# Rounding residues of queries and keys: VectorE for both heads in a hybrid decoder step

## The chip, the cores and the metric

The kernel runs on one core of one Trainium2 chip. The metric is device time in microseconds of one execution of the whole program, from the first instruction to the last; lower is better.

## What is computed

One inference step of a two-layer decoder trunk on 1024 prompt positions and 8 sample positions (1032 columns in all), width 1024, in float32. The first layer mixes tokens with dilated sliding-window attention in three groups of 16 heads, the second with causal pooling; each is followed by a gated MLP with a short convolution. The change lies in the attention of the prompt, which the reference computes per group so:

```python
s = jnp.einsum("nbqhd,nbkhd->nbhqk", qb, kb).astype(jnp.float32) * SCALE
s = s + bias[:, np.clip(rel, 0, SPAN)]
s = jnp.where(valid[None, :, None], s, NEG_INF)
m = jnp.max(s, axis=-1)
p = jnp.exp(s - m[..., None])
l = jnp.sum(p, axis=-1)
o = jnp.einsum("nbhqk,nbkhd->nbqhd", p.astype(v.dtype), vb).astype(jnp.float32)
```

The three groups' outputs are then merged per head, weighted by their softmax denominators, projected and added to the input.

## The kernel before

Activations lie with channels on partitions and positions along the free dimension. Every large product is made of three matmuls in a rounded format (`F32R`): a value is split into a rounded part (hi, a cast) and what the rounding left (lo, a subtraction), and hi x hi, hi x lo and lo x hi are accumulated. Weights are split by `w_split` (L104 cast on ScalarE, L109 subtraction, in the attention stage on GpSimd, in two pieces of 512 columns).

The attention stage runs over 24 units: 8 head pairs, and for each the groups 2, 1, 0. While unit n's queries, keys and values are projected (three weights times three chunks of columns, `accumulate`, L129), unit n-1's attention is woven between the matmuls. A plan of (due time, step) pairs sets the order; its clock is moved by `between()`, once after every three matmuls. Scores (`scores`) are due every 6 ticks from 1, transposes of the exponentials (`probs_t`) from 15, the value product (`pv`) from 24. Each engine works its own queue in order, so the place in the plan is the place in the queue.

What `probs_t` makes is called phl: TensorE transposes the exponentials into the one PSUM bank `pt` (L484, L486), ScalarE casts them (L488), VectorE subtracts (L489). The next transposes need the bank empty, and `pv` (L498, writes `o`) needs phl.

`pack_q` and `pack_k` split a unit's queries and keys for the next unit's scores. A head pair shares 128 partitions, A (the first head, h = 0) the lower 64, B (h = 1) the upper 64. Each works in halves of 512 columns and per head, so each is four steps: `pack_q` is due at 29 and 32 (first half) and at 44.5 and 46.5, `pack_k` at 50, 53, 56 and 59 of the unit's 72 ticks. A step of `pack_q` casts (L407 on ScalarE for the first head, L406 on VectorE for the second) and subtracts (L408); one of `pack_k` casts on VectorE (L417), copies the cast for the other half of the partitions on ScalarE (L418) and subtracts (L419). In the traces the queries are named `x` (the program's own rows `x0`, `x1` are used for them), `x_595` for the first head and `x_596` for the second, the keys `k`.

Other work shares these queues. In the units of an odd head pair (counted from 0) the cached keys of the sample positions are multiplied on GpSimd (L655, `kc`) and summed on VectorE (L644, `sc`); in those of the following even pair the cached values are split (L795 on ScalarE, L796 on GpSimd) and multiplied (L778, `spv`, gathered in `so`, L805). When a head pair's last group is done, `Merge` computes the groups' weights on VectorE (L578 to L586, `me`), TensorE transposes them (L591, `mt`), and GpSimd scales and adds the groups' outputs (L612, L614), in the units of groups 2 and 1 of the next pair. `finish_o` (L534) adds the value products into the output on VectorE. L380 copies the sample columns out of a projection's bank.

Of the kernel before, what the change touches and what calls it, by code (L numbers as in the profile page):

```python
# [11 lines left out]
F32 = mybir.dt.float32  # L12
# [35 lines left out]
def trunk(ctx: ExitStack, tc: tile.TileContext, a, out):  # L48
    nc = tc.nc
# [102 lines left out]
    def x_row(k, dtype=F32):  # L152
        return persist.tile([128, NT], dtype, name=f"x{k}", tag=f"x{k}")
# [137 lines left out]
    with ExitStack() as ph:  # L291
# [9 lines left out]
        keys = [qp.tile([128, 2, T], F32R, name=f"k{h}") for h in range(2)]  # L301
# [95 lines left out]
        queries = []  # L397

        def pack_q(u):

            raw = u.raw[0]
            if not queries:
                queries.extend(x_row(h, F32R)[:, :T] for h in range(2))

            def part(h, own, other, t):
                (nc.vector.tensor_copy(queries[h][own, t], raw[own, t]) if h else  # L406
                 nc.scalar.activation(queries[h][own, t], raw[own, t], AF.Copy))  # L407
                (nc.vector if h else nc.gpsimd).tensor_sub(queries[h][other, t], raw[own, t],  # L408
                                                           queries[h][own, t].bitcast(F32))

            return parts(part, (0, T // 2))

        def pack_k(u):
            raw = u.raw[1]

            def part(h, own, other, t):
                nc.vector.tensor_copy(keys[h][own, 0, t], raw[own, t])  # L417
                nc.scalar.activation(keys[h][other, 0, t], raw[own, t], AF.Copy)  # L418
                (nc.vector if h else nc.gpsimd).tensor_sub(keys[h][own, 1, t], raw[own, t],  # L419
                                                           keys[h][own, 0, t].bitcast(F32))  # L420


            return parts(part, (T // 2, 0))

        def parts(f, starts):
            return [partial(f, h, own, other, slice(t, t + T // 2)) for t in starts
                    for h, (own, other) in enumerate(((A, B), (B, A)))]
# [994 lines left out]
```

## Time and profile before

| what | value |
|---|---|
| median of 3 runs | 2860.18 us (2855.91 to 2860.97) |
| profiled execution | 2860.84 us, span 2859.0 us |
| TensorE (PE) matmul busy | 2778.1 us, 97% of the span |
| VectorE (DVE) busy | 1606.4 us, 56% |
| ScalarE (ACT) busy | 1362.1 us, 48% |
| GpSimd (POOL) busy | 1102.1 us, 39% |
| mean granted TensorE clock | 0.991 |

The shares are means over stages: the attention stage is about the first 1160 us, the rest is projection, pooling and the MLPs. A busy time counts the whole length of an instruction, including time in which it stands still for something that another engine holds. Idle time before an instruction is shown in brackets with what ended it.

### The profile page before, as it was taken

The page shows a single profiled execution, that of the slowest core. Times are in us where ns is not written, and L with a number is a line of the kernel's source. Part 1 is how long each engine was busy: PE and PEld are TensorE (multiplying, and loading weights), DVE is VectorE, ACT ScalarE, POOL GpSimd, SP SyncE. Part 2 cuts the span into 40 slices and gives each one's busy share as a digit, 9 for nine tenths or more (in the row PEclk, how much of TensorE's full clock was granted, in tenths as well). Part 3 has the DMA queues.
Part 4 walks back from the last instruction along what each step waited for, and adds up shares of the span by engine and source line. Part 5 has one row for each costly group of instructions (what it writes and reads, how often), then busy time and mean ns, then how long its engine had stood idle before and what let it go on. Part 6 is the DMA issues. An engine that isn't in the chain of part 4 may idle for free. (4 is left out here: it accounts for less than half of the span.)

```text
span 2859.0 us, 46821 instructions
## 1 busy us (share of the span) xinstructions
PE 2778.1 (97%) x18109; PEld 2741.0 (96%) x18109; DVE 1606.4 (56%) x3335; ACT 1362.1 (48%) x2748; POOL 1102.1 (39%) x982
## 2 busy tenths in 40 slices
PE   7999999999999999999999999999999999999998
PEld 6999999999999999889999999999999999999998
DVE  6566766676666666765333234787755334346655
ACT  5565665566656665634223323445542233334443
POOL 4335453545354535545444443011143443431110
PEclk9999999999999999999999999999999999999999
DMA  3234332433343324437222222333422226223542
GB/s 116 62 83 127 89 98 74 137 88 97 76 136 86 98 74 147 150 93 107 74 67 74 67 68 80 111 118 118 135 87 67 70 73 78 67 75 116 170 144 91
DMA packets 203950, 277.80 MB, mean 97 GB/s; under 512 B 70272, under 2 KB 154096, under 8 KB 203728
## 3 DMA queue, kind: packets, MB, share of 16 engines
q1 hardware_dynamic: 203680, 274.80, 34.3%
q8 instruction: 142, 2.33, 0.3%
q14 instruction: 80, 0.66, 0.1%
q10 hardware_dynamic: 48, 0.02, 0.0%
HBM read 251.89 MB, written 23.34 MB: 96 GB/s over the span
## 5 line engine op out<-in xcount | busy, mean ns | idle before, releaser
L129 PE MATMUL mm<-hh,w_hi 128*128 128x352 f32 (+2 forms) x4064 | 1342.7, 330 | 11.8 <-DVE x L1010 3.8
L129 PE MATMUL mm<-hl,w_hi 128*128 128x352 f32 (+2 forms) x4064 | 1306.4, 321 | 3.9 <-DVE hl L264 2.8
L129 PE MATMUL mm<-hh,w_lo 128*128 128x352 f32 (+2 forms) x4064 | 1306.9, 322 | 2.4 <-DVE w_lo L109 2.4
L129 PEld LDWEIGHTS mm<-hh,w_hi 128*128 128x128 f32 x4064 | 771.2, 190 | 18.4 <-ACT hh L260 4.3
L129 PEld LDWEIGHTS mm<-hl,w_hi 128*128 128x128 f32 x4064 | 772.2, 190 | 5.7 <-DVE hl L264 4.0
L129 PEld LDWEIGHTS mm<-hh,w_lo 128*128 128x128 f32 x4064 | 770.1, 189 | 3.3 <-DVE w_lo L109 3.3
L109 POOL TENSOR_TENSOR w_lo<-w_raw,w_hi 128x512 fp32r<-128x512 f32 (+1 forms) x294 | 532.8, 1824 | 565.5 <-ACT w_hi L104 564.1
L104 ACT ACTIVATE w_hi<-w_raw 128x1024 fp32r<-128x1024 f32 x348 | 364.7, 1050 | 292.1 <-PE mm L129 266.2
L1124 DVE SCALAR_TENSOR_TENSOR conv<-gate,convp,conv 128x336 f32<-128x336 f32 (+1 forms) x176 | 220.4, 1252 | 385.0 <-ACT conv L1122 375.9
L129 PE MATMUL mm<-gh,w_hi 128*128 128x352 f32 (+2 forms) x1056 | 340.6, 322 | 4.0 <-ACT gh L1115 2.1
L129 PE MATMUL mm<-gh,w_lo 128*128 128x352 f32 (+2 forms) x1056 | 339.9, 322 | 2.0 <-DVE w_lo L109 2.0
L129 PE MATMUL mm<-gl,w_hi 128*128 128x352 f32 (+2 forms) x1056 | 340.0, 322 | 0.3 <-POOL gl L1116 0.3
L1062 DVE TENSOR_TENSOR x<-x,mm 128x352 f32<-128x352 f32 (+2 forms) x312 | 157.0, 509 | 226.6 <-PE mm L129 225.9
L476 ACT ACTIVATE p<-p,st 128x128 f32<-128x128 f32 (+1 forms) x384 | 170.0, 443 | 195.9 <-DVE st L473 195.2
L1116 POOL TENSOR_TENSOR gl<-conv,gh 128x352 fp32r<-128x352 f32 (+2 forms) x132 | 123.4, 937 | 339.4 <-ACT gh L1115 336.5
L109 DVE TENSOR_TENSOR w_lo<-w_raw,w_hi 128x1024 fp32r<-128x1024 f32 x136 | 166.5, 1225 | 87.8 <-ACT w_hi L104 87.8
L129 PEld LDWEIGHTS mm<-gh,w_hi 128*128 128x128 f32 x1056 | 199.8, 189 | 4.6 <-ACT gh L1115 2.4
L129 PEld LDWEIGHTS mm<-gh,w_lo 128*128 128x128 f32 x1056 | 200.3, 190 | 2.2 <-DVE w_lo L109 2.2
L129 PEld LDWEIGHTS mm<-gl,w_hi 128*128 128x128 f32 x1056 | 199.9, 189 | 0.7 <-POOL gl L1116 0.7
L489 DVE TENSOR_TENSOR phl<-pt,phl 128x512 fp32r<-128x512 f32 (+1 forms) x192 | 104.6, 545 | 165.8 <-ACT phl L488 164.7
L377 ACT ACTIVATE raw<-mm 128x336 f32<-128x336 f32 (+1 forms) x216 | 145.0, 671 | 102.6 <-PE mm L129 97.5
L1107 ACT ACTIVATE gate<-mm 128x352 f32<-128x352 f32 (+2 forms) x132 | 60.2, 457 | 261.8 <-PE mm L129 261.8
(190 smaller groups left out, 3104.6 us busy)
## 6 DMA issues: line engine op xcount, KB each, us to landing
w_raw<-in_w_in SPq DMA_DIRECT2D x176, 512.0 KB
w_raw<-in_w_out SPq DMA_DIRECT2D x88, 512.0 KB
w_raw<-in_w_qkv SPq DMA_DIRECT2D x72, 512.0 KB
x<-qd SPq DMA_DIRECT2D x48, 256.0 KB
kc<-in_cache_k SPq DMA_DIRECT2D x48, 256.0 KB
vc<-in_cache_v SPq DMA_DIRECT2D x48, 256.0 KB
x<-c_d SPq DMA_DIRECT2D x42, 256.0 KB
out_new_k<-raw SPq DMA_DIRECT2D x8, 516.0 KB
```

The costliest lines, as they stand in the source:

```text
L104: nc.scalar.activation(hi, raw, AF.Copy)
L109: eng.tensor_sub(lo[:, s:s + step], raw[:, s:s + step], hi[:, s:s + step].bitcast(F32))
L129: nc.tensor.matmul(ps, l, r, start=first and i == 0, stop=last and i == n - 1)
L377: nc.scalar.activation(stream(raw[:, :T], u.g, c0, t1, which > 0), ps[:, :w].rearrange("p (s r) -> p s r", r=DILS[u.g]), AF.Copy, scale=si ...
L476: nc.scalar.activation(p[:, h, :w], p[:, h, :w], AF.Exp, bias=u.st[:, i, h, 0:1], scale=-1.0, accum_out=u.st[:, i, h, 1:2])
L489: nc.vector.tensor_sub(phl[:, :, 1, :w], ps[:, :, :w], phl[:, :, 0, :w].bitcast(F32))
L1062: nc.vector.tensor_add(xT[ct][:, c0:c1], xT[ct][:, c0:c1], ps)
L1107: nc.scalar.activation(gate[:, 2 + s:2 + e], group(tiles8(w, c), c), AF.Copy)
L1116: nc.gpsimd.tensor_sub(self.gl[f][:, s:e], conv[:, s:e], self.gh[f][:, s:e].bitcast(F32))
L1124: nc.vector.scalar_tensor_tensor(conv[:, :n], gate[:, j:j + n], cw[j], conv[:, :n], op0=ALU.mult, op1=ALU.add)
```

## The change

The subtractions of the first head in `pack_q` and `pack_k`, 48 and 48 of them, are issued on VectorE instead of GpSimd. The casts stay where they were.

```diff
             def part(h, own, other, t):
                 (nc.vector.tensor_copy(queries[h][own, t], raw[own, t]) if h else
                  nc.scalar.activation(queries[h][own, t], raw[own, t], AF.Copy))
-                (nc.vector if h else nc.gpsimd).tensor_sub(queries[h][other, t], raw[own, t],
-                                                           queries[h][own, t].bitcast(F32))
+                nc.vector.tensor_sub(queries[h][other, t], raw[own, t], queries[h][own, t].bitcast(F32))
...
                 nc.vector.tensor_copy(keys[h][own, 0, t], raw[own, t])
                 nc.scalar.activation(keys[h][other, 0, t], raw[own, t], AF.Copy)
-                (nc.vector if h else nc.gpsimd).tensor_sub(keys[h][own, 1, t], raw[own, t],
-                                                           keys[h][own, 0, t].bitcast(F32))
+                nc.vector.tensor_sub(keys[h][own, 1, t], raw[own, t], keys[h][own, 0, t].bitcast(F32))
```

The order on TensorE, ScalarE and the DMA queue is the same in both; line numbers past L408 are one or two lower in the changed kernel. VectorE's queue, while the queries' second half and the keys of the last head pair's group 1 are packed (the stretch from 1101 us), before (`sc` is the sums of the sample's scores, `k_100` the first head's keys, `k_101` the second's):

```order
L534 TENSOR_TENSOR x_12532<-o,part 64x4x64 x2
L489 TENSOR_TENSOR phl<-pt,phl 128x2x128
L380 TENSOR_SCALAR ks<-mm 128x8
L406 CAST x_596<-raw 64x512
L408 TENSOR_TENSOR x_596<-raw,x_596 64x512
L644 TENSOR_REDUCE sc<-kc 128x2x2 x2
L417 CAST k_100<-raw 64x512
L489 TENSOR_TENSOR phl<-pt,phl 128x2x128
L417 CAST k_101<-raw 64x512
```

and now:

```order
L532 TENSOR_TENSOR x_12532<-o,part 64x4x64 x2
L408 TENSOR_TENSOR x_595<-raw,x_595 64x512
L487 TENSOR_TENSOR phl<-pt,phl 128x2x128
L380 TENSOR_SCALAR ks<-mm 128x8
L406 CAST x_596<-raw 64x512
L408 TENSOR_TENSOR x_596<-raw,x_596 64x512
L642 TENSOR_REDUCE sc<-kc 128x2x2 x2
L416 CAST k_100<-raw 64x512
L418 TENSOR_TENSOR k_100<-raw,k_100 64x512
L487 TENSOR_TENSOR phl<-pt,phl 128x2x128
L416 CAST k_101<-raw 64x512
```

A subtraction of the first head now stands ahead of each phl subtraction.

GpSimd's queue in the same stretch, before:

```order
L614 TENSOR_TENSOR x_10954<-x_10954,x_11970 128x512
L655 TENSOR_TENSOR kc<-kc,x_12437 128x512
L408 TENSOR_TENSOR x_595<-raw,x_595 64x512
L109 TENSOR_TENSOR w_lo<-w_raw,w_hi 128x512 x2
L655 TENSOR_TENSOR kc<-kc,x_12437 128x512
L419 TENSOR_TENSOR k_100<-raw,k_100 64x512
L655 TENSOR_TENSOR kc<-kc,x_12437 128x512
L419 TENSOR_TENSOR k_100<-raw,k_100 64x512
```

and now:

```order
L612 TENSOR_TENSOR x_10954<-x_10954,x_11970 128x512
L653 TENSOR_TENSOR kc<-kc,x_12437 128x512
L109 TENSOR_TENSOR w_lo<-w_raw,w_hi 128x512 x2
L653 TENSOR_TENSOR kc<-kc,x_12437 128x512 x2
L109 TENSOR_TENSOR w_lo<-w_raw,w_hi 128x512 x4
```

The weight split and the cache products close up behind one another; the second weight split, which waits for ScalarE, follows.

## Rows read from the trace of the kernel before

**Rows 1.** TensorE's waits, 85 to 1160 us: waiter, waited for; total us, times, longest.

```profile
PE mt L591 <- DVE me L586: 8.4, 4, 2.1
PE spv L778 <- DVE so L805: 5.9, 6, 1.4
PE o L498 <- DVE phl L489: 5.1, 5, 2.0
PE pt L484 <- DVE phl L489: 1.9, 5, 0.5
```

**Rows 2.** The two changed lines: engine, count; ns min/median/max; first and last start; form.

```profile
L408 POOL TENSOR_TENSOR x<-raw,x x48: 1275/1288/1717, 64.0 to 1145.6; 64x512 fp32r<-64x512 f32 x48
L408 DVE TENSOR_TENSOR x<-raw,x x48: 686/687/1673, 65.6 to 1147.3; 64x512 fp32r<-64x512 f32 x48
...
L419 POOL TENSOR_TENSOR k<-raw,k x48: 1266/1450/1752, 72.0 to 1157.6; 64x512 fp32r<-64x512 f32 x48
L419 DVE TENSOR_TENSOR k<-raw,k x48: 687/1652/1679, 72.4 to 1160.1; 64x512 fp32r<-64x512 f32 x48
```

**Rows 3.** Timeline from 1101 us, VectorE, GpSimd, TensorE: start, length, operation [idle before].

```profile
1101.38 0.42 DVE L489 TENSOR_TENSOR phl<-pt,phl 128x256 fp32r<-128x256 f32 x1 [0.38 <-ACT phl L488]
...
1102.25 0.47 DVE L406 CAST x<-raw 64x512 fp32r<-64x512 f32 x1
1102.76 1.66 DVE L408 TENSOR_TENSOR x<-raw,x 64x512 fp32r<-64x512 f32 x1
...
1105.09 0.76 DVE L417 CAST k<-raw 64x512 fp32r<-64x512 f32 x1
1105.77 0.41 DVE L489 TENSOR_TENSOR phl<-pt,phl 128x256 fp32r<-128x256 f32 x1
...
1111.71 0.42 DVE L489 TENSOR_TENSOR phl<-pt,phl 128x256 fp32r<-128x256 f32 x1
...
1101.15 1.28 POOL L612 TENSOR_TENSOR x<-x,x 128x512 f32<-128x512 f32 x1
1102.51 1.35 POOL L614 TENSOR_TENSOR x<-x,x 128x512 f32<-128x512 f32 x1
1103.83 1.74 POOL L655 TENSOR_TENSOR kc<-kc,x 128x512 f32<-128x512 f32 x1
...
1107.08 3.07 POOL L109 TENSOR_TENSOR w_lo<-w_raw,w_hi 128x512 fp32r<-128x512 f32 x2
...
1106.68 0.38 PE L484 MATMUL pt<-consts,p 128*128 128x128 f32 x2
...
1112.19 0.55 PE L498 MATMUL o<-phl,vhl 128*128 128x128 f32 x3 [0.41 <-DVE phl L489]
```

**Rows 4.** Timeline from 395 us, VectorE, GpSimd, TensorE, columns as above.

```profile
396.21 1.40 DVE L417 CAST k<-raw 64x512 fp32r<-64x512 f32 x1
397.54 0.41 DVE L489 TENSOR_TENSOR phl<-pt,phl 128x256 fp32r<-128x256 f32 x1
...
395.71 3.05 POOL L109 TENSOR_TENSOR w_lo<-w_raw,w_hi 128x512 fp32r<-128x512 f32 x2
...
398.01 0.44 PE L484 MATMUL pt<-consts,p 128*128 128x128 f32 x2 [0.20 <-DVE phl L489]
```

**Rows 5.** Busy us by stretch: PE, PEld, DVE, ACT, POOL, granted clock; one wait.

```profile
197.00:211.00 14.00, 11.93 (x81) 11.64 (x80) 13.22 (x29) 7.39 (x14) 8.30 (x6) 0.99 0.37 110
289.00:305.00 16.00, 16.00 (x110) 15.96 (x109) 15.18 (x27) 8.68 (x20) 11.28 (x10) 1.00 0.32 93
439.00:451.00 12.00, 12.00 (x83) 11.99 (x82) 9.34 (x13) 5.99 (x14) 4.82 (x4) 1.00 0.26 68
...
210.60:214.00 3.40, 3.40 (x14) 3.40 (x14) 1.57 (x8) 2.47 (x7) 1.50 (x2) 0.50 0.43 163
...
209.49 0.29 PE L591 MATMUL mt<-consts,me 128*48 128x128 f32 x1 [2.07 <-DVE me L586]
```

**Rows 6.** The first unit's keys, timeline of VectorE and TensorE.

```profile
72.43 1.63 DVE L419 TENSOR_TENSOR k<-raw,k 64x512 fp32r<-64x512 f32 x1
...
74.21 0.55 PE L464 MATMUL s<-k,x 128*128 128x256 f32 x1 [0.26 <-DVE k L419]
```

## The prediction

> **What bounds the kernel now.** I read first the busy time by stretch, then what TensorE waits for, then the instructions around those waits. Between 439 and 451 us TensorE is busy for all of 12.00 us [rows 5]: in the attention stage, from 85 to 1160 us, where the changed lines run, it is the bound, so a delay elsewhere costs time only when TensorE reaches a matmul whose operand isn't ready. The list of TensorE's waits in that stage is short: 8.4 us in four waits for the merge weights, 5.9 us for the sample sums, 5.1 and 1.9 us for the rounded probabilities (phl), all made by VectorE [rows 1]. None is for GpSimd's subtractions. So taking those off GpSimd opens nothing on TensorE's path in this stage; what counts is whether VectorE, which already ends every wait, gets later.
>
> It has little room. In a unit of an odd head pair it is busy 13.22 of 14 us, or 15.18 of 16, while keys are packed; in a unit of an even pair without sample or merge work 9.34 of 12 [rows 5].
>
> **Price of one subtraction.** The four rows of the two lines say it [rows 2]: on GpSimd 1.28 us at best, 1.29 and 1.45 in the median; on VectorE 0.69 at best, but up to 1.68, and the key line's median is 1.65. The long ones are those that start while a GpSimd operation runs: the two engines take turns. In the unit at 394 us the cast at 396.21 takes 1.40 us behind the first piece of GpSimd's weight split (two pieces from 395.71 in 3.05 us), where a cast alone takes 0.47 [rows 3, 4]. The order is by turns too: when VectorE finishes one such instruction and GpSimd has one waiting, GpSimd goes next (the cast of 1102.25 ends at 1102.72, GpSimd's operation of 1102.51 then runs to 1103.86, and the subtraction behind the cast, from 1102.76, takes 1.66 us [rows 3]). So the 96 moved subtractions cost VectorE between 0.69 and 0.69 + 1.28 us each, and what they give back is the wait that GpSimd's own subtraction used to cause, up to 1.68 - 0.69 = 0.99 us each. One at a time that is anything from -0.3 to +2.0 us; the place decides, by what VectorE has next in its queue and what GpSimd has ready.
>
> The Trainium skill, "SBUF — State Buffer", section "Who interferes with whom", says that a VectorE instruction with two inputs in SBUF and a GpSimd instruction that reads SBUF share a port, which the one that comes first holds for its whole length while the other blocks. The rows at 396.21 agree. The page alone would also speak for this change: 0.69 us of holding replaces 1.28; that result is the second rival below.
>
> **The change, place by place.** Each of the 24 units (a head pair and a group) has four subtractions of the first head: two query halves and two key halves. The first query half comes some 10 us before the rest; the other three fall into the crowded stretch. The program's order on TensorE, ScalarE and the DMA queue stays; on VectorE each first-head subtraction is put directly behind its cast, ahead of the phl subtraction that TensorE waits for.
>
> *Odd pairs, group 1 (four units).* I walk the one at 1101 us [rows 3]. Now: phl done at 1101.80; second query cast done 1102.72; its subtraction 1104.42; first key cast 1105.85; phl 1106.18, half a microsecond ahead of the transposes at 1106.68, which need that PSUM bank empty. Then: the new query subtraction takes its turn before GpSimd's operation of 1101.15, ends at 1101.9, phl at 1102.35. GpSimd's operation slides to 1103.2, the cast behind it ends at 1103.6 (0.9 late); GpSimd's next takes until 1104.9, the second head's subtraction ends at 1105.6 (1.2 late); the cache product of 1103.83 now runs to 1106.9, the key cast ends at 1107.3 (1.5 late). The weight split is next and takes its first piece, to 1108.6; only then the new key subtraction, to 1109.3, and phl, to 1109.7: 3.5 us late, 3.0 more than TensorE's slack. At the next phl (now done at 1112.13, with a wait of 0.41) the second new key subtraction and one more GpSimd turn make VectorE 4.3 us late in all. The walk gives +4.3; I take 3.5, since it has every GpSimd operation ready the moment the removed ones leave its queue, and some need a transfer. 4 x 3.5 = 14.0 us.
>
> *Even pairs after the first, group 1 (three units).* Now: cast until 397.61, phl until 397.95, transposes at 398.01 already wait 0.20 [rows 4]. Then: behind the cast the second weight piece goes first (1.28), to 398.9; the new subtraction ends at 399.6, phl at 400.0. 2.0 us late, nothing in between: 3 x 2.0 = 6.0 us.
>
> *Odd pairs, group 2 (four units).* The merge weights stand on VectorE right behind the key packing, and TensorE already waits 2.07 us for them at 209.49 [rows 5]. Two new key subtractions come ahead of them; I let the waits saved and the waits added cancel: 2 x 0.69 = 1.4, four times: 5.6 us.
>
> *Odd pairs, group 0 (four units).* No wait now, at 15.18 of 16 us busy [rows 5]. The same two subtractions find no room: 4 x 1.4 = 5.6 us.
>
> *The rest.* In units like that at 439 us three subtractions, 2.1 us, fit into 12 - 9.34 = 2.7 us of idle time: nothing. The units with sample products I put at nothing too; they have idle time at the places where the new ones stand.
>
> *The first unit.* Here TensorE does wait for the packing: its second score matmul starts at 74.21, when VectorE's 1.63 us subtraction of 72.43 is done [rows 6]. With GpSimd out of the way both heads' take 2 x 0.69 = 1.4: -0.3 us.
>
> A new wait comes with the move: VectorE, in order, now waits for ScalarE's cast of the first head's queries before it subtracts, and phl, the second head's cast and the score reductions queue behind it. That cast stands ahead of the one that phl itself waits for on ScalarE, so I price it at nothing; if it came last, it would add to the group 1 units.
>
> Sum: 14.0 + 6.0 + 5.6 + 5.6 - 0.3 = 30.9 us. The profiled execution took 2860.84 us (span 2859.0), 0.7 above the median of 2860.18: about 2891 us by the median, 1.1% slower.
>
> **Rivals.** *Worse than that.* The walk's full 4.3 in group 1 of the odd pairs, and in all seven group 1 units the first query half makes one more turn, 1.0 us: 4 x (4.3 + 1.0) + 3 x (2.0 + 1.0) = 30.2 in place of 20.0. On top, TensorE's clock: after the 2.07 us wait at 209.49 the granted clock in 210.6 to 214.0 is 0.50, the level of 1.2 GHz [rows 5], so 1.7 us of its work is lost; seven new waits of some 2 us would add 12. Together 2860 + 31 + 10 + 12 = 2913 us. For it: the turns are in the rows. Against it: not every wait of 2 us need bring the clock down, and a slow TensorE gives VectorE time. Chance 0.15.
>
> *Faster.* One mechanism: in the crowded stretches the shared turns, not VectorE's own work, set when VectorE is done, and a removed GpSimd subtraction gives back 0.97 us (1.66 against 0.69 in the second head's query subtraction at 1102.76 [rows 3]) for 0.69 spent. Then three per unit gain 0.84 us in the 15 units above: -12.6, well within TensorE's waits of 21.3 us [rows 1], so 2847 us. It decides from the point where a removed subtraction saves VectorE more than 0.69 us on average. Against it: GpSimd has other work ready in its place (from 1101.15 on its operations follow with hardly a gap), so the turn isn't given back but taken by the next operation. The port rule of the page named above would put the gain higher, since it compares 1.28 with 0.69; the rows speak for the turn being used by others. Chance 0.10.
>
> *No difference.* Given back and spent cancel within 0.2% (5.7 us, about what a measurement of this kernel can tell from no change): if only the even pairs' group 1 units lose, 2860 + 6 - 0.3 = 2866, or less. It needs VectorE's lateness to be made good before TensorE asks; the half microsecond of slack at 1106.18 speaks against it. Chance 0.12.
>
> **How the numbers follow.** Forecast 2891 us, chance 0.63, with its own range from 2867 (0.2% above, where each unit loses what its slack lets through) to 2905. Range: 2861 leaves out the faster case and a little of the second; 2914 takes in the worse case's sum. Faster by over 0.2%: 0.10; within: 0.12; slower: 0.63 + 0.15 = 0.78.
>
> **What would show it.** In the changed kernel's trace: VectorE's subtractions of both lines, 96 each, GpSimd's gone; TensorE's waits for phl, now 7.0 us in ten, over 20 us, with waits of 2 to 4 us at the transposes of group 1 units; the four waits for merge weights near 3.5 us each, in one piece or shared with a wait for phl just ahead; no new wait in even pairs' group 0. If TensorE's waits for phl stay near 7 us while VectorE's busy time in the crowded stretches doesn't grow, the turns were given back and the forecast is wrong. If VectorE waits for ScalarE's query cast for more than a few microseconds in all, I priced that at nothing wrongly.

## The result, and the profile after

The changed kernel takes 2876.09 us in the median of four runs (2874.05 to 2881.04), against 2859.18 us for four runs of the kernel before beside it: a ratio of 1.006, 95% interval 1.0044 to 1.0076. It is slower by 0.6%, 17 us; the forecast was 31 us. The profiled execution took 2874.05 us with a span of 2872.2 us, 13.2 more than the span of before; where the other 4 us of the medians' distance lie no trace shows.

TensorE's waits in the attention stage, 85 to 1175 us of the changed kernel (waiter, what it waited for; total us, times, longest), against [rows 1]:

```profile
PE pt L482 <- DVE phl L487: 19.5, 19, 2.4
PE spv L776 <- DVE so L803: 7.1, 6, 1.8
PE o L496 <- DVE phl L487: 4.8, 5, 1.9
PE mt L589 <- DVE me L584: 3.1, 4, 0.8
```

(Line numbers after the change are one or two lower than before.) The waits for phl at the transposes have gone from 1.9 us to 19.5; the four for the merge weights have fallen from 8.4 us to 3.1. The two changed lines, now VectorE's alone (count; ns min/median/max), and what VectorE waited for ahead of the first, against [rows 2]:

```profile
L408 DVE TENSOR_TENSOR x<-raw,x x96: 684/687/1797, 64.1 to 1160.9; 64x512 fp32r<-64x512 f32 x96
its engine sat idle before it (us, times) until:
  ACT x L407: 5.2, 15
...
L418 DVE TENSOR_TENSOR k<-raw,k x96: 682/690/1675, 71.6 to 1173.2; 64x512 fp32r<-64x512 f32 x96
```

The key subtraction's median was 1652 ns before and is 690 now. The engines' busy time (page of the changed kernel):

```profile
PE 2779.5 (97%) x18109; PEld 2738.2 (95%) x18109; DVE 1645.1 (57%) x3431; ACT 1363.3 (47%) x2748; POOL 980.8 (34%) x886
```

VectorE has 96 instructions more and is busy 38.7 us longer (1606.4 before), 0.40 us for each new one, less than the 0.69 us that one takes alone. So part of the new work was paid by waits that VectorE no longer has. A unit with merge weights shows it instruction by instruction. First the kernel before, from 196.9 us (start, length, operation): the four key casts of VectorE with their subtractions, then GpSimd.

```profile
197.49 1.01 DVE L417 CAST k<-raw 64x512 fp32r<-64x512 f32 x1
199.13 0.81 DVE L417 CAST k<-raw 64x512 fp32r<-64x512 f32 x1
199.97 1.67 DVE L419 TENSOR_TENSOR k<-raw,k 64x512 fp32r<-64x512 f32 x1
203.18 1.13 DVE L417 CAST k<-raw 64x512 fp32r<-64x512 f32 x1
204.80 1.15 DVE L417 CAST k<-raw 64x512 fp32r<-64x512 f32 x1
205.99 0.69 DVE L419 TENSOR_TENSOR k<-raw,k 64x512 fp32r<-64x512 f32 x1
...
201.06 1.74 POOL L419 TENSOR_TENSOR k<-raw,k 64x512 fp32r<-64x512 f32 x1
204.39 1.27 POOL L419 TENSOR_TENSOR k<-raw,k 64x512 fp32r<-64x512 f32 x1 [0.36 <-DVE k L417]
```

Then the same unit of the changed kernel, VectorE, GpSimd and TensorE:

```profile
196.99 0.96 DVE L416 CAST k<-raw 64x512 fp32r<-64x512 f32 x1
197.99 1.68 DVE L418 TENSOR_TENSOR k<-raw,k 64x512 fp32r<-64x512 f32 x1
199.59 0.67 DVE L487 TENSOR_TENSOR phl<-pt,phl 128x512 fp32r<-128x512 f32 x1
200.29 0.79 DVE L416 CAST k<-raw 64x512 fp32r<-64x512 f32 x1
201.12 0.69 DVE L418 TENSOR_TENSOR k<-raw,k 64x512 fp32r<-64x512 f32 x1
...
203.34 0.42 DVE L416 CAST k<-raw 64x512 fp32r<-64x512 f32 x1
203.80 0.68 DVE L418 TENSOR_TENSOR k<-raw,k 64x512 fp32r<-64x512 f32 x1
204.97 0.42 DVE L416 CAST k<-raw 64x512 fp32r<-64x512 f32 x1
205.43 0.69 DVE L418 TENSOR_TENSOR k<-raw,k 64x512 fp32r<-64x512 f32 x1
...
211.97 1.29 POOL L109 TENSOR_TENSOR w_lo<-w_raw,w_hi 128x512 fp32r<-128x512 f32 x1 [9.00 <-ACT w_hi L104]
...
200.32 0.44 PE L482 MATMUL pt<-consts,p 128*128 128x128 f32 x2 [1.05 <-DVE phl L487]
208.94 0.29 PE L589 MATMUL mt<-consts,me 128*48 128x128 f32 x1 [0.78 <-DVE me L584]
```

Before, six instructions took 1.01 + 0.81 + 1.67 + 1.13 + 1.15 + 0.69 = 6.46 us. After, eight take 0.96 + 1.68 + 0.79 + 0.69 + 0.42 + 0.68 + 0.42 + 0.69 = 6.33. The two subtractions added were paid in full by the casts, which no longer stand behind GpSimd's subtraction; GpSimd had nothing to put in its place (idle for 9.00 us until 211.97). Only the order within VectorE's queue is worse: the first new subtraction takes 1.68 us ahead of phl, and TensorE waits 1.05 us for that, but 0.78 for the merge weights in place of 2.07 [rows 5].

In a unit of group 1 of an odd pair the walk on record came nearer. This is the unit of [rows 3], which now lies some 13 us later:

```profile
1115.35 3.16 POOL L109 TENSOR_TENSOR w_lo<-w_raw,w_hi 128x512 fp32r<-128x512 f32 x2
...
1116.62 0.76 DVE L416 CAST k<-raw 64x512 fp32r<-64x512 f32 x1
1117.41 1.64 DVE L418 TENSOR_TENSOR k<-raw,k 64x512 fp32r<-64x512 f32 x1
1118.98 0.41 DVE L487 TENSOR_TENSOR phl<-pt,phl 128x256 fp32r<-128x256 f32 x1
...
1119.44 0.44 PE L482 MATMUL pt<-consts,p 128*128 128x128 f32 x2 [2.39 <-DVE phl L487]
1125.78 0.55 PE L496 MATMUL o<-phl,vhl 128*128 128x128 f32 x3 [1.19 <-DVE phl L487]
```

Cast and subtraction each give one piece of GpSimd's weight split its turn, phl comes last, and TensorE waits 2.39 us.

### The profile page after: what moved, and what is told of

Its sections match the earlier page's. It is cut to its first block, busy times and chain, and to the rows that moved or that the text cites. A ratio compares the mean times of both kernels' runs of the same rounds, so it can differ in the third digit from the quotient of the medians.

```text
span 2872.2 us, 46751 instructions
## 1 busy us (share of the span) xinstructions
PE 2779.5 (97%) x18109; PEld 2738.2 (95%) x18109; DVE 1645.1 (57%) x3431; ACT 1363.3 (47%) x2748; POOL 980.8 (34%) x886
```

## The experiments

The theory: **VectorE reaches phl late** because the new subtractions stand ahead of it, and the forecast's size is off because it let nothing come back from GpSimd. The rivals: GpSimd fills its turns anyway, so nothing comes back (B); the cost is VectorE's new wait for ScalarE's cast of the queries (C); the cost is spread over all units alike (D). Beside the times stand two sums for each profiled execution, worked out from its trace: all gaps of 0.1 us or more between TensorE's matmuls, and the time lost to a lower granted clock, span x (1 - mean clock), known to about 1.5 us.

| kernel | median us | ratio to before (95%) | TensorE gaps | clock | VectorE busy |
|---|---|---|---|---|---|
| before | 2857 to 2859 | 1 | 63.0 | 26 | 1606.4 |
| after | 2876.09 | 1.0060 (1.0044 to 1.0076) | 74.9 | 26 | 1645.1 |
| left out on both engines | 2845.00 | 0.9949 (0.9936 to 0.9961) | 52.1 | 23 | 1565.7 |
| on both engines | 2915.09 | 1.0205 (1.0191 to 1.0219) | 103.7 | 38 | 1705.9 |
| twice on VectorE | 2940.09 | 1.0282 (1.0267 to 1.0297) | 122.5 | 50 | 1721.1 |
| queries only | 2861.93 | 1.0013 (1.0002 to 1.0023) | 65.5 | 23 | 1632.5 |
| keys only | 2882.45 | 1.0084 (1.0068 to 1.0099) | 78.7 | 32 | 1619.3 |

**Both sides of the change apart.** The first run takes the work away in all units but the first:

```diff
-                nc.vector.tensor_sub(keys[h][own, 1, t], raw[own, t], ...)
+                if h or (u.hp, u.g) == (0, 2):
+                    (nc.vector if h else nc.gpsimd).tensor_sub(keys[h][own, 1, t], raw[own, t], ...)
```

and the same for the queries.

> The first head's residue subtractions of queries and keys are done in the first unit only (by GpSimd, as before) and left out in the other 23 units, whose first head then works with the residues of the first unit. So neither engine spends time on them: the run stands between the two kernels and splits their 17 us (2859 to 2876) in what the removal from GpSimd gives back and what the addition to VectorE costs. Theory A (the turns that GpSimd's own subtractions took are given back to VectorE, and the forecast erred in letting nearly none come back): 2848 to 2855 us, TensorE's waits in attention down from 22 to under 17 us, and the addition alone costs more than 20 us. Rival B (GpSimd fills the turns with other work, as the forecast said, nothing comes back): 2857 to 2860 us, and the addition costs 17 us, half of the forecast only because VectorE's slack was larger than my walk had it.

Measured: 2845.0 us, 13 us below before and 31 below the changed kernel. TensorE's waits, 85 to 1175 us:

```profile
PE mt L593 <- DVE me L588: 2.4, 4, 0.6
...
PE pt L486 <- DVE phl L491: 1.0, 3, 0.4
```

Theory A holds, with more coming back than expected. Taking 92 subtractions off GpSimd, with VectorE's instructions unchanged in number, made VectorE busy 40.7 us less: those were waits for GpSimd (39 of the 40.7 us are in the casts and subtractions of queries and keys). Rival B falls.

The counterpart leaves GpSimd's work in and adds VectorE's:

```diff
+                if not h:
+                    nc.gpsimd.tensor_sub(spare[own], raw[own, t], keys[h][own, 0, t].bitcast(F32))
                 nc.vector.tensor_sub(keys[h][own, 1, t], raw[own, t], keys[h][own, 0, t].bitcast(F32))
```

and the same for the queries.

> The changed kernel, and GpSimd subtracts the first head's queries and keys as well, at its old place, into a spare buffer of half-width numbers that nobody reads. So VectorE has its 96 new subtractions and GpSimd's 96 have not gone: this is the sum on record as it was made, with nothing given back. Theory A (the forecast's price of adding was right and its error is that it let nothing come back): what leaving GpSimd's work out gave (13 us) is lost again, 2876 + 13 = 2889, from 2885 to 2895 us; VectorE busy 1675 us or more (1645 in the changed kernel, and GpSimd's presence was worth 41 us of it where it was left out). Rival B (GpSimd fills its turns with other work anyway): 2874 to 2880 us, VectorE busy within 10 us of 1645.

Measured: 2915.09 us, VectorE busy 1705.9. TensorE's waits, 80 to 1200 us:

```profile
PE pt L488 <- DVE phl L493: 28.1, 26, 2.4
PE o L502 <- DVE phl L493: 10.4, 9, 1.5
PE mt L595 <- DVE me L590: 7.9, 4, 2.0
```

Its span and mean granted clock (0.991 in the kernels before and after):

```profile
core 0: 2913.1 us, clock 0.987
```

The direction is A's, the size beyond it. The four corners, by the ratios times 2859 us: adding the subtractions to VectorE costs 32 us when GpSimd doesn't do them (0.9949 to 1.0060), but 59 us when it does (1 to 1.0205); taking them from GpSimd gives 15 us when VectorE doesn't have them (1 to 0.9949), but 41 when it does (1.0205 to 1.0060). The change is +59 - 41, or -15 + 32. The 59 and the 41 are both somewhat too high: GpSimd's key subtraction into the spare buffer takes 1.44 us at its shortest, against 1.27 in [rows 2] (the queries' 1.28 as before), and no run separates what that costs. TensorE's gaps alone give the same picture, 23 and 41 us for adding, 11 and 29 for removing; the rest of the 59 is mostly the granted clock (26 to 38).

**More of the same work.** Each first-head subtraction is issued twice on VectorE:

```diff
+                for _ in range(1 if h else 2):
                     nc.vector.tensor_sub(keys[h][own, 1, t], raw[own, t], ...)
```

and the same for the queries.

> The changed kernel with every subtraction of the first head issued twice in a row on VectorE (same result): 96 more at 0.69 us alone. The second one removes nothing from GpSimd, so nothing can come back. Theory A (the first ones were made cheap by the turns given back): dearer than the first, 25 us or more in units of group 1 (7 units x 3 x 0.69 = 14.5) and in units with merge weights and group 0 of odd pairs (8 x 2 x 0.69 = 11): 2896 to 2912 us. Rival B (no give-back; what is paid is VectorE's time less its slack): about as dear as the first or, with the slack used up, the same 0.69 apiece: 2890 to 2896 us. Under 2885 us neither holds and the busy time of VectorE isn't what costs.

Measured: 2940.09 us, 64 above the changed kernel; VectorE busy 76.0 us longer, 0.79 for each of the 96. One line of TensorE's waits from 85 to 1175 us shows where it went:

```profile
PE pt L484 <- DVE phl L489: 59.0, 32, 4.1
```

Above what either theory expected: the second 96 cost nearly four times what the change does. Nothing comes back for them, and little of VectorE's slack is left; some 18 of the 64 us are TensorE's own matmuls at a lower clock (busy 2797.7 us against 2779.5). Units of even pairs in which TensorE never waited now wait too (7.5 us of gaps in five).

**Queries and keys apart.** Each of these two undoes one line of the changed kernel, the keys' first, then the queries'.

```diff
-                nc.vector.tensor_sub(keys[h][own, 1, t], raw[own, t], ...)
+                (nc.vector if h else nc.gpsimd).tensor_sub(keys[h][own, 1, t], raw[own, t], ...)
```

> VectorE subtracts only the queries of the first head; the keys stay on GpSimd. Theory A (VectorE is late for the rounded probabilities because of the two key subtractions that stand directly ahead of them; the query subtraction comes earlier and is partly made good): 2859 to 2865 us, at most a third of the 17 us. Rival C (the cost is VectorE's new wait for ScalarE's cast of the queries, 5.2 us in all in the trace of the changed kernel, and what queues behind it): 2868 to 2876 us, two thirds or more of it.

```diff
-                nc.vector.tensor_sub(queries[h][other, t], raw[own, t], ...)
+                (nc.vector if h else nc.gpsimd).tensor_sub(queries[h][other, t], raw[own, t], ...)
```

> VectorE subtracts only the keys of the first head; the queries stay on GpSimd. Theory A: 2868 to 2876 us, two thirds or more of the 17 us, and TensorE's waits for the rounded probabilities at the transposes 10 us or more. Rival C (ScalarE's cast of the queries is what VectorE waits for): 2859 to 2863 us.

Measured: queries 2861.93 us, keys 2882.45. TensorE's waits from 85 to 1175 us, first with the queries moved:

```profile
PE o L497 <- DVE phl L488: 4.1, 5, 1.5
PE pt L483 <- DVE phl L488: 4.0, 8, 0.7
```

then with the keys moved:

```profile
PE pt L483 <- DVE phl L488: 17.0, 11, 2.1
...
PE o L497 <- DVE phl L488: 4.8, 6, 1.6
```

The keys carry the waits for phl, as theory A had it. Rival C falls: the run with the queries alone has the whole new wait for ScalarE (5.2 us in 15 waits, as in the changed kernel) and costs 3.7 us. The keys alone cost more than the expected 2868 to 2876, and more than keys and queries together. Of the 8.3 us between the two profiled spans (2880.5 and 2872.2), the gaps hold 3.8 (units with merge weights and group 1 of even pairs wait longer while GpSimd still has queries) and the granted clock about the rest; the two ratios' intervals overlap, so the order of the two isn't settled.

**Places.** VectorE has the first head in even pairs' units only:

```diff
-                (nc.vector if h else nc.gpsimd).tensor_sub(...)
+                (nc.vector if h or u.hp % 2 == 0 else nc.gpsimd).tensor_sub(...)
```

> VectorE subtracts the first head's queries and keys in units of even head pairs only; in odd pairs (group 1, the merge weights, group 0) GpSimd has them as before. Theory A (the cost sits where VectorE has no room, in odd pairs and in the even pairs' group 1): the gaps of TensorE that grew in even pairs are 1.0 us in three group 1 units, 0.4 in three sample units: 2859 + 4 = 2863, from 2859 to 2867 us. Rival D (the cost is spread over all units, by 0.7 us for each unit): half of 17, 2868 us.

Measured: 2864.57 us, ratio 1.0027 (1.0018 to 1.0036), 7 us where 4 was expected and D had 8.5, so the time alone doesn't decide. The gaps do: group 1 of even pairs 6.02 us in three units (5.98 in the changed kernel, 2.57 before), their sample units 6.44 (6.46, and 5.20 before), the other units of even pairs nothing. The cost has places, and D falls.

**Same work, other place.** The residues are needed by the next unit's scores only, so the subtractions can stand behind the unit's last phl. Casts and subtractions become separate steps of the plan, and three quarters of the subtractions of both heads go later:

```diff
+                    subs = (29, 29 + 3, 59.5, 60.5) if i == 2 else (57.5, 58.5, 65.5, 67)
-                    plan.extend(zip(places, pack_q(u) if i == 2 else pack_k(u)))
+                    for when, fs in zip((places, subs), pack_q(u) if i == 2 else pack_k(u)):
+                        plan.extend(zip(when, fs))
```

> The changed kernel with the casts where they are, but all subtractions of both heads except the first query half put later, most of them behind the last rounded probabilities of the unit (places 57.5 to 67 in the plan in place of 44.5 to 59). Same work on VectorE, the same turns. Theory A (what costs is that TensorE waits for probabilities rounded behind the subtractions): TensorE's waits at the transposes fall from 19.5 to under 5 us and the time to 2848 to 2860 us. Rival B (VectorE is simply short of time in these units): the lateness moves to the merge weights and to the next unit's first scores, which need the residues, and the time stays at 2870 to 2885 us.

> The kernel before with the same later places, the first head's subtractions on GpSimd. Theory A: TensorE's waits for rounded probabilities and merge weights (15.4 us in all) fall to under 6 us: 2845 to 2853 us, faster than both kernels; if it is slower than the late version on VectorE, the change itself is good once its place is right. Rival B: 2858 to 2870 us, since the first scores of the next unit wait for GpSimd's last key subtraction.

Measured: on VectorE 2863.82 us, ratio 1.0022 (1.0013 to 1.0031); on GpSimd 2873.27, 1.0053 (1.004 to 1.0065). TensorE's waits from 80 to 1200 us of the late version on VectorE:

```profile
PE mt L593 <- DVE me L588: 6.2, 4, 1.7
PE spt L803 <- DVE ct L595: 5.3, 3, 1.8
PE mm L129 <- ACT raw L382: 4.8, 1, 4.8
PE mt L593 <- DVE spv_sb L785: 4.2, 3, 1.4
...
PE pt L486 <- DVE phl L491: 1.5, 4, 0.4
```

The waits for phl at the transposes are gone (19.5 to 1.5), so the place ahead of phl was their cause, and VectorE has the time (busy 1613.1 us with all 192 subtractions, 32 less than in the changed kernel). The second head's subtractions moved along, though, and this run doesn't separate the two heads; that the waits were nearly as short before the change (1.9 us), with the second head's in their early places, speaks for the first head's. The late places stand ahead of the merge weights and sample transposes, which wait longer, and in the last unit one wait of 4.8 us is for ScalarE's copy of the sample columns (L382). The expectation for GpSimd failed: there the late places made it slower than before, not faster. With late places VectorE is the better engine, the other way round than with the early ones.

From these comes a version by unit: late places on VectorE, but sample units (group 2 of head pairs 2, 4 and 6) as before the change, with GpSimd, and the last unit as after it. Behind it a variant with later places in the units with merge weights, and the same by unit with GpSimd everywhere (its only edit is the engine).

```diff
+                    subs = places
+                    if not sampled(u) and n < len(order) - 1:
+                        subs = (29, 29 + 3, 59.5, 60.5) if i == 2 else (57.5, 58.5, 65.5, 67)
```

> The late version on VectorE, except in the three units with sample products (group 2 of even pairs after the first), where the late places cost 2.2 us each (the merge weights and sample transposes behind them wait longer) and which go back to the kernel before (early places, first head on GpSimd), and the last unit, which keeps the changed kernel's places. Theory A (each class of units keeps the wait that it had in the run it is taken from): TensorE's waits from the second unit on are 4 x 1.5 for the merge weights, 5 for group 1 of odd pairs, 3 x 1.7 for the sample units, 2 for group 1 of even pairs, 2 for the last: 20 us against 24 in the kernel before and 27 in the late version, so 2850 to 2857 us, faster than both. Rival (the gaps saved return as waits elsewhere or as a lower granted clock): 2858 to 2864 us.

```diff
+                        if u.g == 2:
+                            subs = (29, 29 + 3, 70.5, 71) if i == 2 else (68, 69, 65, 66.5)
```

> As the run before, and in the units with merge weights (group 2 of odd pairs) the late subtractions stand behind the merge weights (places 65 to 71 in place of 57.5 to 67). Theory A (the merge weights wait for whatever stands ahead of them on VectorE): the four waits fall from 1.5 to 0.6 us or less, the value where these subtractions were partly left out: 3 to 4 us faster than the run before, 2846 to 2854 us. Rival: the next unit's first scores wait for the residues instead, 1 to 2 us in each of the four units: as fast as the run before or up to 5 us slower.

> The first of these three runs with the first head's subtractions on GpSimd in all units, so that places alone differ from the kernel before. From the classes of the two late runs: merge weights 4 x 2.5, group 1 of odd pairs nothing, sample units 3 x 1.7, even pairs' group 1 three times 0.5, the last 3: 20 us of waits, the same as on VectorE. Theory A (place decides, not engine): within 5 us of the first of these runs, 2850 to 2858 us. Rival (engine decides: GpSimd's subtractions still take VectorE's turns, as in the late pair, where it cost 9 us): 8 us or more slower than the first of these runs.

Measured: 2854.51 us, 0.9987 (0.9978 to 0.9996); behind the merge weights 2853.67, 0.9984 (0.9976 to 0.9993); by unit on GpSimd 2860.53, 1.0004 (0.9995 to 1.0013). The first two beat both kernels, by some 5 us against before and 22 against after; they can't be told from each other. In the second of them TensorE no longer waits for the merge weights, but, as its rival had it, for the residues (85 to 1170 us):

```profile
PE s L469 <- DVE k L425: 4.4, 8, 1.0
```

On GpSimd the version by unit is 6 us slower than on VectorE, between what the two theories expected, and the intervals just overlap. The merge weights wait longer on GpSimd; here is that line from the waits of 85 to 1170 us, on VectorE and then on GpSimd:

```profile
PE mt L596 <- DVE me L591: 6.5, 4, 1.8
...
PE mt L596 <- DVE me L591: 10.9, 4, 3.0
```

Other waits are shorter, so that TensorE's gaps are the same: 62.8 us on VectorE, 61.7 on GpSimd. What differs is the clock. From 200 to 1100 us the granted clock falls to 0.50 for 3.4 us at a time, once on VectorE, seven times on GpSimd, there behind each wait of 2.4 to 3.0 us for the merge weights and behind three of 1.4 us for the sample sums; TensorE's same matmuls are busy 2773.3 and 2782.9 us. Nor do shorter waits show as what the version on VectorE gains against the kernel before, whose gaps are 63.0 us: its matmuls are busy 4.8 us less (2778.1 before). These are single profiled executions; over the eleven runs of each, the mean granted clock is 0.991 on VectorE and 0.989 on GpSimd.

## Why the prediction was right, and where its sizes were not

Right: the sign, the bound and the mechanism. TensorE waits for VectorE, no wait was for GpSimd, and the new waits are for phl at the transposes, as named: 19.5 us there and 24.3 us in all, where over 20 was forecast. The longest in each unit of group 1 is 1.3 to 2.4 us, not 2 to 4. Even pairs' group 0 got no new wait, as said. The four waits in the units with merge weights came to 1.8 us each, shared between phl and merge weights, not to 3.5. The size was nearly twice too large: 31 us against 17. The gaps of TensorE by class of unit show which terms failed. Each number is the sum over the class, in us, in the trace of one profiled execution; the columns "left out" and "on both" are the two one-sided kernels:

| class of units | before | left out | on both | after | after - before | forecast |
|---|---|---|---|---|---|---|
| odd pairs, group 1 (4) | 4.60 | 0.57 | 14.96 | 12.75 | +8.2 | +14.0 |
| even pairs, group 1 (3) | 2.57 | 2.66 | 8.82 | 5.98 | +3.4 | +6.0 |
| odd pairs, group 2, merge weights (4) | 8.36 | 2.37 | 16.29 | 7.24 | -1.1 | +5.6 |
| odd pairs, group 0 (4) | 3.48 | 0.62 | 10.65 | 3.43 | -0.1 | +5.6 |
| sample units (3) | 5.20 | 5.20 | 6.49 | 6.46 | +1.3 | 0 |
| first unit | 11.24 | 13.00 | 14.89 | 10.66 | -0.6 | -0.3 |
| the rest | 27.57 | 27.68 | 31.61 | 28.39 | +0.8 | 0 |

**The step that failed** is "I let the waits saved and the waits added cancel", in the units with merge weights and in group 0 of odd pairs. It priced two subtractions at 1.4 us in each of eight units, 11.2 us; measured is -1.2. In the units with merge weights the saved waits paid for the subtractions themselves too: 6.46 us of packing became 6.33 in the unit shown above, and in all four it takes VectorE 0.13 to 0.20 us less than before. So the 13.22 of 14 us busy were no measure of VectorE's room there: the four casts and the subtraction of 199.97 took 5.77 us of them, and alone take 4 x 0.42 + 0.69 = 2.37. The rival "faster" had that mechanism and put its threshold at 0.69 us given back for each; these four units reach it. What spoke against it, that GpSimd has other work ready, was read off one unit, the one from 1101 us, and holds there (GpSimd's operations from 1109.73 to 1120.18 follow with hardly a gap); in the unit from 197 us GpSimd stood idle instead.

Group 0 of odd pairs is another case. Packing the keys takes VectorE 0.22 to 0.90 us longer there, so 0.24 to 0.58 us came back for each new subtraction, and the three earlier units wait 0.3 to 0.5 us more, all for phl. The class comes to nothing because the last unit waits 1.3 us less: a wait of 2.03 us for ScalarE's copy of the sample columns (L382), at 1165.22 before, is gone. Why it is gone stays open.

**Group 1 of odd pairs** had the right place and mechanism, but was mis-sized: 2.0 us a unit, not 3.5. The four differ: +0.3, +2.5, +1.9 and +3.5; the walked unit is the last, and its +3.5 matches the 3.5 taken from the walk. I walked the worst unit and multiplied it by four. The first of them already waited 2.5 us before the change, which may be why it gained so little more; no run shows that. **Group 1 of even pairs**: phl comes late as walked, but 1.1 us a unit, not 2.0. **Sample units**: I had put them at nothing; each waits 0.42 us longer. **The first unit** came out as said in kind: two waits on VectorE's keys in place of one on GpSimd's and one on VectorE's,

```profile
72.46 0.35 PE L462 MATMUL s<-k,x 128*128 128x256 f32 x1 [1.88 <-DVE k L418]
73.64 0.49 PE L462 MATMUL s<-k,x 128*128 128x256 f32 x1 [0.83 <-DVE k L418]
```

2.71 us in all against 3.17. **ScalarE's query cast**, priced at nothing: VectorE waits 5.2 us for it, more than the few that the prediction set as its sign of a wrong price; the whole cost of the run with the queries alone is 3.7 us (0.6 to 6.6 by its interval). **The clock**: nothing lost to it, as the likeliest case had it; the "worse" rival's 12 us appear in the run with the work on both engines instead (26 to 38).

**The sum as I made it** let nothing come back, except that in the eight units of the failed step saved waits paid for added ones, and the run on both engines is the nearest that the chip has to it. It measures +59 us, not +31. So the price of adding was too low and the give-back far too low; the two errors had opposite signs, and the forecast landed in its range by their partial cancelling, not by the sum. The price was not too low everywhere: from "before" to "on both" group 1 of odd and of even pairs grows by 10.4 and 6.2 us, where the forecast had 14.0 and 6.0, and what the sum lacks lies in the units with merge weights and group 0 of odd pairs (15.1 against 11.2), in the classes put at nothing, and in the clock. The change's gaps account for 11.9 us of the 13.2 between the two profiled spans.

The Trainium skill, "SBUF — State Buffer", section "Who interferes with whom", says that the holder of the shared port keeps it for its whole instruction. That fits what was measured: taking 92 of GpSimd's instructions away shortened VectorE's by 40.7 us in the run that leaves them out. The row of 396.21, which the prediction set beside the page's sentence, is a cast, with one input; an instruction with two is the subtraction of 1102.76 [rows 3], 1.66 us where it takes 0.69 alone. What the prediction drew from the rule, shorter holding and so a gain, does not hold for this kernel (+0.6%), since the rule says nothing of where in VectorE's queue the new instruction stands.

## What to carry to other kernels

A move of work between two engines that take turns has two prices, adding here and removing there, and they aren't independent: measure or bound each with the other present. Ask of each place whether the relieved engine has other work ready; a walk through one unit says nothing of the units where it would stand idle. And before choosing the engine, put the instruction behind what the bound engine waits for: here later places on VectorE (with GpSimd kept in three of the 24 units) turned a loss of 17 us into a gain of 5. And look at the clock beside the waits: two versions with the same gaps differed by 6 us.

## What the runs showed of the hardware

That VectorE's busy time can hold so much waiting was unexpected: with the first head's subtractions off GpSimd, the same number of VectorE instructions took 40.7 us less, and a unit's last two key casts fell from 1.13 and 1.15 us to 0.42 (203.18 and 204.80 before, 203.34 and 204.97 after).

And equal waits don't cost an equal clock. In the changed kernel TensorE waited 2.40 us at 247.26 and 2.39 us at 1119.44, at the same place of two units of one class; the stretches behind them (busy us by engine, then granted clock):

```profile
1119.40:1122.80 3.40, 3.36 (x24) 3.36 (x25) 3.32 (x6) 1.02 (x2) 0.79 (x1) 1.00 0.81 253
247.80:251.20 3.40, 3.40 (x15) 3.40 (x14) 3.32 (x7) 0.95 (x2) 0.94 (x2) 0.50 1.00 334
```

One was followed by 3.4 us at 0.50, the level of 1.2 GHz, and the other by none, so 1.7 us of a single wait's cost is there in one unit and not in the other.
